# Another place for the split weights, one for each pair of gate and up groups

## The chip, the cores and the metric

The kernel runs on one core of a Trainium2 chip. The metric is the device time of one execution in microseconds (us). A profile of one execution shows TensorE (PE for its matmuls, PEld for its weight loads), VectorE (DVE), ScalarE (ACT), GpSimd (POOL) and the DMA queue of SyncE (SP).

## What is computed

Two layers of a hybrid block on one sequence of 256 tokens with 2,048 features, in float32. Each layer does an input projection, three mixers side by side (a spatial gate, a sliding-window attention and an mLSTM), an output projection, and a gated feed-forward block with 5,632 hidden features:

```
def hybrid_layer(x, ...):
    hn = rmsnorm(x, norm1_g)
    proj = hn @ w_in
    a_u, a_v, b_q, b_k, b_v, c_qk, c_v, c_o, c_i, c_f = jnp.split(proj, split_idx, axis=-1)
    ...
    mixed = jnp.concatenate([mix_a, mix_b, mix_c], axis=-1)
    h = x + mixed @ w_out
    hn2 = rmsnorm(h, norm2_g)
    return h + (jax.nn.silu(hn2 @ w_gate) * (hn2 @ w_up)) @ w_down
```

A last `rmsnorm` follows the second layer.

## The kernel before

**Products in two parts.** Every float32 weight and every activation is split into a high part (rounded to the type float32r, which TensorE multiplies in one pass) and a low part, the remainder. A product is the sum of high times high, high times low and low times high. The weights come from HBM in chunks of 4 x 128 rows by 512 columns. `wsplit` takes half a chunk (1,024 words of each partition): ScalarE writes the high part (`wh`, L206) and then VectorE subtracts it from the raw weight and writes the low part (`wl`, L207). Each of the two tiles `wh` and `wl` has four blocks of 1,024 words (`NSPLIT` = 4), used in turn; a block can be written again when the matmuls that read it have ended.

**Three forms.** Each product (a "group": 512 output columns over all the rows of the weight) is one call of `gemm` in one of three forms. In form A the activation is the stationary operand and the weights' part, 512 columns of it, is moved through the array (L262 to L264: three matmuls for each 128 rows and each half of the tokens). In forms B and C a 128 x 128 piece of the weights' part is stationary and the activation is moved. Form C uses two matmuls for a piece: L280 with the high part of the weights against 512 columns (both parts of the activation), and L281 with the low part against 256 columns. I call the two a pair. While one matmul runs, the stationary operand of the next one is loaded. Form B (L284 to L286) has three matmuls of 256 columns.

**Who uses which.** In each layer the groups run in this order: conv inputs `G_CQ` and `G_CK` (form B in layer 0, C in layer 1), the small group of 264 columns (A), `G_CV`, `G_Q0`, `G_Q1`, `G_AV` (A), `G_AU` (B), `G_CO` (A), 4 groups of the output projection (C), then twice: gate and up groups (12 the first time, 10 the second; C) and 4 groups of the down projection (C, but A the last time in layer 1). The 22 gate and up groups of a layer have 64 pairs each. Two consecutive ones are a "pair of groups", 11 of them, numbered 0 to 10 here.

**Places.** Within each block the parts don't begin at word 0 but at an offset that depends on the form alone, in words of 4 bytes, first for `wh`, then for `wl`:

```
LINE = 32
PLACE = dict(A=(20, 20), B=(12, 12), C=(24, 28))
```

The built program puts `wh` at byte 108,672 and `wl` at byte 125,184 of each partition, the activation `xn_sb` at 35,712, the four `big` tiles (which hold gated activations) at 141,696, 192,128, 200,320 and 208,512, and ten `slot` tiles every 4,224 bytes from 149,888. Counted modulo 256 bytes, `xn_sb` and all `big` tiles begin at 128, the slots by turns at 128 and 0; the blocks of `wh` and `wl` in form C at 224 and 112, in form A at 208 and 80. Where a product reads activations from slots, the profile's rows name them `slot`. In the first down projection of layer 1 the first two slots that are read begin at 128, the other two at 0, modulo 256; in the second down projection of layer 0 the two slots that are read begin at 0 and 128, two pairs each by turns; in the last down projection of layer 1 both begin at 0.

**Order.** Splits are issued with a high priority, and the scheduler puts each instruction into its engine's queue when what it depends on is scheduled. Dependences are found by the words that instructions read and write.

Of the kernel before, what the change touches and what calls it, by code (L numbers as in the profile page):

```python
# [8 lines left out]
F32R = mybir.dt.float32r  # L9
# [4 lines left out]
P = 128  # L14
# [13 lines left out]
CW = 512  # L28
WK = 4
SK = 2  # L30
# [9 lines left out]
LINE = 32  # L40
PLACE = dict(A=(20, 20), B=(12, 12), C=(24, 28))
NSPLIT = 4
# [6 lines left out]
OFF = dict(a_u=0, a_v=512, b_q=1024, b_k=2048, b_v=2176, c_q=2304, c_k=2816, c_v=3328, c_o=3840, c_i=4352, c_f=4356)  # L49
G_CQ, G_CK, G_CV, G_Q0, G_Q1, G_AV, G_AU, G_CO = range(8)  # L50
GROUP_COLS = [OFF["c_q"], OFF["c_k"], OFF["c_v"], OFF["b_q"], OFF["b_q"] + 512, OFF["a_v"], OFF["a_u"], OFF["c_o"]]


_p = 0
# [18 lines left out]
def hybrid(ctx: ExitStack, tc: tile.TileContext, xt, wfirst, win, wsm, wout, wgu, wdn, prm, cst, fgb, yt):  # L73
# [8 lines left out]
    wp = ctx.enter_context(tc.tile_pool(name="wp", bufs=1))  # L82
# [32 lines left out]
    def bank():  # L115
        return pm.tile([P, 512], F32, tag="m", name=nm("m"))
# [5 lines left out]
    def kchunks(w, order=None):  # L122

        order = range(KT // WK) if order is None else order
        return [(w[c], list(range(c * WK, (c + 1) * WK))) for c in order]
# [66 lines left out]
            load_next()  # L192
        return loaded[i]

    parts = [wp.tile([P, NSPLIT * SK * CW + LINE], F32R, tag=k, name=k) for k in ("wh", "wl")]
    split_no = [0]
    last_split = [None]

    def wsplit(raw, lo, n, form, pieces=1):
        i = split_no[0] % NSPLIT  # L200
        split_no[0] += 1
        wh, wl = [t[:, i * SK * CW + o:(i + 1) * SK * CW + o] for t, o in zip(parts, PLACE[form])]
        m = n // pieces
        with tc.high_priority(HIPRI):
            for i in range(0, n, m):
                A.copy(wh[:, i:i + m], raw(lo + i, m))  # L206
                last_split[0] = V.tensor_tensor(wl[:, i:i + m], raw(lo + i, m), wh[:, i:i + m].bitcast(F32),  # L207
                                                op=ALU.subtract)
        return wh, wl
# [9 lines left out]
    def gemm(*args, **kw):  # L219

        steps = gemm_steps(*args, **kw)
        while True:
            try:
                next(steps)
            except StopIteration as end:
                return end.value
# [9 lines left out]
                    out[i] = end.value  # L236
        return [out[i] for i in range(len(steps))]

    def gemm_steps(form, chunks, xs, cols=CW, ready=None, step0=SK, split=0):

        ps = [bank(), bank()] if split else gbank()
        if form == "C":
            up = [bank(), bank()]
            tiles = [ps[:, 0:512], ps[:, 512:1024], up[0], up[1]]  # L250
        nk = sum(len(k) for _, k in chunks)
        done = 0

        def mm_a(wh, wl, j, kt, first, last, cs=range(NC)):
            xh, xl = xs(kt)
            h = wh[:, j * cols:(j + 1) * cols]
            lo = wl[:, j * cols:(j + 1) * cols]
            for c in cs:
                o = ps[c][:, 0:cols] if split else ps[:, c * 512:c * 512 + cols]
                xhc = xh[:, c * P:(c + 1) * P]  # L260
                xlc = xl[:, c * P:(c + 1) * P]
                T.matmul(o, xhc, h, start=first, stop=False)  # L262
                T.matmul(o, xhc, lo, start=False, stop=False)  # L263
                T.matmul(o, xlc, h, start=False, stop=last)  # L264

        def mm_first(wh, wl, kt):

            xh, xl = xs(kt)
            for i, (w, x) in enumerate(((wh, xh), (wh, xl), (wl, xh))):
                for f in range(4):  # L270
                    T.matmul(ps[:, f * S:(f + 1) * S], w[:, f * P:(f + 1) * P], x, start=i == 0 and f % 2 == 0,
                             stop=False, skip_group_check=True)

        def mm_f(wh, wl, j, kt, f, first, last):
            xh, xl = xs(kt)
            h = wh[:, j * CW + f * P:j * CW + (f + 1) * P]
            lo = wl[:, j * CW + f * P:j * CW + (f + 1) * P]
            if form == "C":
                o = tiles[f]
                T.matmul(v3(o, 2), h, xs(kt, True), start=first, stop=False, skip_group_check=True)  # L280
                T.matmul(o[:, 0:S], lo, xh, start=False, stop=last, skip_group_check=True)  # L281
            else:
                o = ps[:, f * S:(f + 1) * S]
                T.matmul(o, h, xh, start=first and f % 2 == 0, stop=False, skip_group_check=True)  # L284
                T.matmul(o, h, xl, start=False, stop=False, skip_group_check=True)  # L285
                T.matmul(o, lo, xh, start=False, stop=last, skip_group_check=True)  # L286

        second = []
        for ci, (src, kts) in enumerate(chunks):
            apart = ci >= len(chunks) - split  # L290
            raw, step = wload(src, len(kts) * cols), step0 if ci == 0 else SK
            late = form != "A" and ci == len(chunks) - 1
            held = []
            for s0 in range(0, len(kts), step):
                ks = kts[s0:s0 + step]
                wh, wl = wsplit(raw, s0 * cols, len(ks) * cols, form, 2 if done == 0 and ready is ready_x else 1)
                if ready is not None:
                    ready(ks)
                for j, kt in enumerate(ks):
                    first, last = done == 0, done == nk - 1  # L300
                    done += 1
                    if form == "A":
                        mm_a(wh, wl, j, kt, first, last, range(1) if apart else range(NC))
                        if apart:
                            second.append((wh, wl, j, kt, first, last))
                    elif late:
                        held.append((wh, wl, j, kt, first, last))
                    elif first and ready is ready_x:
                        mm_first(wh, wl, kt)
                    else:  # L310
                        for f in range(4):
                            mm_f(wh, wl, j, kt, f, first, last)
                if not late:
                    pump()
                if step0 == 1 and ci == 0 and s0 + step < len(kts):
                    yield
            if late:
                for f in range(4):
                    for wh, wl, j, kt, first, last in held:
                        mm_f(wh, wl, j, kt, f, first, last)  # L320
                    if f % 2 == 1:
                        pump()
            if ci < len(chunks) - 1:
                yield
        for a in second:
            mm_a(*a, range(1, NC))
        return (ps, up[0], up[1]) if form == "C" else ps
# [29 lines left out]
    for g in range(2):  # L357
        for d in range(2):
            o = slice((1 - d) * HD, (2 - d) * HD)
# [632 lines left out]
    for l in range(DEPTH):  # L992
# [1 line left out]
        st = {}  # L994

        def inproj(i, form):
            return gemm(form, kchunks(win[l, i]), xn)

        if l == 0:
            start(rstd_of(st, True))  # L1000
            ps, ps1 = in_turn(gemm_steps("B", kchunks(win[l, G_CQ]), xn, ready=ready_x, step0=1),
                              gemm_steps("B", kchunks(win[l, G_CK]), xn, step0=1))
        else:
            start(rstd_of(st))
            ps = inproj(G_CQ, "C")
# [3 lines left out]
        ps = ps1 if l == 0 else inproj(G_CK, "C")  # L1009
        start(conv(st, "kc", scaled_in(ps, rbc), pr("conv"), 4))  # L1010
        ks, vn, gt = small_in(gemm("A", kchunks(wsm[l]), xn, cols=SMALL), rstd, pr)
# [10 lines left out]
        ps = inproj(G_AU, "B")  # L1022
        mixed[0] = big()
        start(gmlp_u(st, ps, rbc, mixed[0]))
        ps = inproj(G_CO, "A")
# [19 lines left out]
        for half, (c0, c1) in enumerate(HALVES):  # L1045
# [3 lines left out]
            for g in range(ng):  # L1049
                if half == 0 and g == 0:  # L1050
                    st = {}
                    start(rstd_of(st))
                ps = gemm("C", kchunks(wgu[l, 2 * c0 + g]), xn)
                need(st, "rbc")
                rbc = st["rbc"]
                ts = slot()
                t = ts[:, 0:1024]
                joined(t, ps)
                V.tensor_tensor(v3(t, 4), v3(t, 4), bc4(rbc), op=ALU.mult)
                A.activation(t[:, 0:512], t[:, 0:512], AF.Silu)  # L1060
                V.tensor_tensor(t[:, 0:512], t[:, 0:512], t[:, 512:1024], op=ALU.mult)
                if g >= 2 * NBIG:
                    a = slot(F32R)
                    small_act.append(a)
                    av = a[:, 0:1024].rearrange("p (k i t) -> p k i t", k=2, i=2)
                else:
                    if g % 2 == 0:
                        pair = big()
                    av = pair[:, 2 * (g % 2):2 * (g % 2) + 2]
                A.copy(av[:, :, 0, :], v3(t[:, 0:512], 2))  # L1070
                V.tensor_tensor(av[:, :, 1, :], v3(t[:, 0:512], 2), av[:, :, 0, :].bitcast(F32), op=ALU.subtract)
                release(ts)
                act.append(av)
# [112 lines left out]
```

## Time and profile before

| what | us |
|---|---|
| median of 3 runs (lowest, highest) | 2096.72 (2096.36, 2098.51) |
| the profiled execution | 2095.96 |
| its span, first to last instruction | 2094.1 |
| PE busy in it | 2081.6 |
| DVE busy | 1352.4 |
| ACT busy | 1022.9 |

The profiled execution is 1.9 us longer than its span (work around the program), and 0.8 us shorter than the median. The mean granted clock of TensorE was 0.999 of full speed. A row of the timeline gives the start of a matmul in us from the span's start; matmuls overlap in the array, so what one costs is read from start to start, not from its duration.

### The profile page before, as it was taken

How to read it: one execution, taken by the hardware profiler on the slowest of the kernel's cores; microseconds unless marked ns; L12 is line 12 of the kernel's file. 1: busy time of each engine (PE TensorE's matmuls, PEld its weight loads, DVE VectorE, ACT ScalarE, POOL GpSimd, SP SyncE). 2: the span in 40 equal slices, each digit the busy share in tenths (PEclk: the TensorE clock that was granted, in tenths of full speed). 3: DMA queues.
4: the chain of work that ended last, by engine and by line, in shares of the span. 5: the costliest groups of instructions: out<-in, count | busy, mean ns of one | idle time of the engine just before them, and what ended most of it. 6: DMA issues, size and time to landing. Idle time of an engine off the chain costs nothing.

```text
span 2094.1 us, 29478 instructions
## 1 busy us (share of the span) xinstructions
PE 2081.6 (99%) x12004; PEld 1824.8 (87%) x12004; DVE 1352.4 (65%) x1876; ACT 1022.9 (49%) x1350; POOL 9.1 (0%) x14
## 2 busy tenths in 40 slices
PE   9999999999999999999999999999999999999998
PEld 9888888888888888888888888888888888888886
DVE  7776666656654556566677865765665555656695
ACT  5665545444443345444455654454544434445443
POOL 0000000000000000000000000000000000000000
PEclk9999999999999999999999999999999999999999
DMA  6544555555555555555545435555555555555553
GB/s 253 210 144 148 181 188 194 185 197 184 199 187 195 182 200 183 199 183 200 185 160 199 144 138 192 190 188 195 187 195 193 189 191 191 196 186 196 206 194 128
DMA packets 56296, 390.47 MB, mean 186 GB/s; under 512 B 6496, under 2 KB 7008, under 8 KB 10080
## 3 DMA queue, kind: packets, MB, share of 16 engines
q1 hardware_dynamic: 55872, 388.06, 52.1%
q8 instruction: 94, 1.54, 0.3%
q10 hardware_dynamic: 288, 0.52, 0.1%
q14 instruction: 42, 0.34, 0.0%
HBM read 386.47 MB, written 2.10 MB: 186 GB/s over the span
## 4 chain that ended last, share of the span: by engine, by line
PE 98%; ACT 1%; DVE 0%; issue 0%; DMA 0%; SPq 0%; POOLq 0%; POOL 0%; DVEq 0%; ACTq 0%
PE g L280 25%; PE m L280 25%; PE g L281 13%; PE m L281 13%; PE g L262 5%; PE g L263 5%; PE g L264 5%; PE g L284 1%; PE g L286 1%; PE g L285 1%; PE m L608 1%; PE m L662 1%; PE m L651 1%; PE m L262 0%; PE m L263 0%; PE m L264 0%
## 5 line engine op out<-in xcount | busy, mean ns | idle before, releaser
L207 DVE TENSOR_TENSOR wl<-raw,wh 128x1024 fp32r<-128x1024 f32 (+2 forms) x741 | 886.5, 1205 | 579.3 <-ACT wh L206 576.1
L206 ACT CAST wh<-raw 128x1024 fp32r<-128x1024 f32 (+2 forms) x741 | 758.7, 1034 | 816.6 <-PE m L280 577.7
L280 PE MATMUL g<-xn_sb,wh 128*128 128x512 f32 x1472 | 534.8, 390 | 0.0
L280 PE MATMUL m<-xn_sb,wh 128*128 128x512 f32 x1472 | 533.7, 390 | 0.0
L281 PE MATMUL g<-xn_sb,wl 128*128 128x256 f32 x1472 | 409.6, 278 | 0.0
L281 PE MATMUL m<-xn_sb,wl 128*128 128x256 f32 x1472 | 409.6, 278 | 0.0
L280 PEld LDWEIGHTS m<-xn_sb,wh 128*128 128x128 f32 x1472 | 276.3, 188 | 58.0
L280 PEld LDWEIGHTS g<-xn_sb,wh 128*128 128x128 f32 x1472 | 276.3, 188 | 57.9
L281 PEld LDWEIGHTS g<-xn_sb,wl 128*128 128x128 f32 x1472 | 276.3, 188 | 0.2
L281 PEld LDWEIGHTS m<-xn_sb,wl 128*128 128x128 f32 x1472 | 276.3, 188 | 0.0
L280 PE MATMUL g<-big,wh 128*128 128x512 f32 x640 | 234.2, 390 | 0.0
L280 PE MATMUL m<-big,wh 128*128 128x512 f32 x640 | 233.9, 390 | 0.0
L281 PE MATMUL g<-big,wl 128*128 128x256 f32 x640 | 178.3, 279 | 0.0
L281 PE MATMUL m<-big,wl 128*128 128x256 f32 x640 | 178.3, 279 | 0.0
L262 PE MATMUL g<-wh,xn_sb 128*128 128x512 f32 (+1 forms) x384 | 146.5, 381 | 0.0
L263 PE MATMUL g<-wl,xn_sb 128*128 128x512 f32 (+1 forms) x384 | 144.2, 376 | 0.0
L264 PE MATMUL g<-wh,xn_sb 128*128 128x512 f32 (+1 forms) x384 | 143.4, 373 | 0.0
L280 PEld LDWEIGHTS m<-big,wh 128*128 128x128 f32 x640 | 120.2, 188 | 25.5
L280 PEld LDWEIGHTS g<-big,wh 128*128 128x128 f32 x640 | 120.2, 188 | 25.4
L281 PEld LDWEIGHTS g<-big,wl 128*128 128x128 f32 x640 | 120.2, 188 | 0.1
L281 PEld LDWEIGHTS m<-big,wl 128*128 128x128 f32 x640 | 120.2, 188 | 0.0
L264 PEld LDWEIGHTS g<-wh,xn_sb 128*128 128x128 f32 x384 | 72.3, 188 | 13.9
(238 smaller groups left out, 2098.7 us busy)
## 6 DMA issues: line engine op xcount, KB each, us to landing
raw<-in_wgu SPq DMA_DIRECT2D x176, 1024.0 KB, 4.7
raw<-in_wdn SPq DMA_DIRECT2D x88, 1024.0 KB, 4.7
raw<-in_win SPq DMA_DIRECT2D x62, 1024.0 KB, 4.8
raw<-in_wout SPq DMA_DIRECT2D x32, 1024.0 KB, 4.7
raw<-in_wsm SPq DMA_DIRECT2D x8, 528.0 KB, 3.2
out_yt<-end SPq DMA_DIRECT2D x4, 384.0 KB, 3.0
raw<-in_wfirst SPq DMA_DIRECT2D x2, 512.0 KB, 6.9
hT<-in_xt SPq DMA_DIRECT2D x1, 1024.0 KB, 14.2
```

The source lines that it names most:

```text
L206: A.copy(wh[:, i:i + m], raw(lo + i, m))
L207: last_split[0] = V.tensor_tensor(wl[:, i:i + m], raw(lo + i, m), wh[:, i:i + m].bitcast(F32), op=ALU.subtract)
L262: T.matmul(o, xhc, h, start=first, stop=False)
L263: T.matmul(o, xhc, lo, start=False, stop=False)
L264: T.matmul(o, xlc, h, start=False, stop=last)
L280: T.matmul(v3(o, 2), h, xs(kt, True), start=first, stop=False, skip_group_check=True)
L281: T.matmul(o[:, 0:S], lo, xh, start=False, stop=last, skip_group_check=True)
L284: T.matmul(o, h, xh, start=first and f % 2 == 0, stop=False, skip_group_check=True)
L285: T.matmul(o, h, xl, start=False, stop=False, skip_group_check=True)
L286: T.matmul(o, lo, xh, start=False, stop=last, skip_group_check=True)
L608: T.matmul(o, q2[d][:, sl], k[:, 0:n], start=i == 0, stop=i == 1, skip_group_check=True)
L651: T.transpose(b[:, p * P:(p + 1) * P], pslice(c, 2 * p + par)[:, blk * P:(blk + 1) * P], ident)
```

## The change

It gives a place of its own to each pair of gate and up groups (`GU_PLACE`, the same in both layers) and to ten groups of form A (`A_PLACE`, five in each layer). All other groups keep `PLACE`. `wl` gets 64 more words at its end, so that every tile that stands behind it (slots, `big` tiles, small tiles) moves up by 256 bytes.

```diff
+GU_PLACE = ((24, 60), (24, 44), (24, 92), (23, 28), (25, 28), (24, 27), (24, 29), (25, 29), (23, 27), (22, 26), (20, 24))
+A_PLACE = ({G_CV: (32, 32), G_Q0: (19, 19), G_Q1: (20, 32), G_AV: (32, 20), G_CO: (31, 31)},
+           {G_CV: (30, 30), G_Q0: (18, 20), G_Q1: (20, 84), G_AV: (20, 52), G_CO: (0, 0)})
...
-    parts = [wp.tile([P, NSPLIT * SK * CW + LINE], F32R, tag=k, name=k) for k in ("wh", "wl")]
+    parts = [wp.tile([P, NSPLIT * SK * CW + n * LINE], F32R, tag=k, name=k) for k, n in (("wh", 1), ("wl", 3))]
...
-    def wsplit(raw, lo, n, form, pieces=1):
+    def wsplit(raw, lo, n, place, pieces=1):
...
-        wh, wl = [t[:, i * SK * CW + o:(i + 1) * SK * CW + o] for t, o in zip(parts, PLACE[form])]
+        wh, wl = [t[:, i * SK * CW + o:(i + 1) * SK * CW + o] for t, o in zip(parts, place)]
...
-    def gemm_steps(form, chunks, xs, cols=CW, ready=None, step0=SK, split=0):
+    def gemm_steps(form, chunks, xs, cols=CW, ready=None, step0=SK, split=0, place=None):
...
-                wh, wl = wsplit(raw, s0 * cols, len(ks) * cols, form, 2 if done == 0 and ready is ready_x else 1)
+                wh, wl = wsplit(raw, s0 * cols, len(ks) * cols, place or PLACE[form], 2 if done == 0 and ready is ready_x else 1)
...
-            return gemm(form, kchunks(win[l, i]), xn)
+            return gemm(form, kchunks(win[l, i]), xn, place=A_PLACE[l].get(i))
...
-                ps = gemm("C", kchunks(wgu[l, 2 * c0 + g]), xn)
+                ps = gemm("C", kchunks(wgu[l, 2 * c0 + g]), xn, place=GU_PLACE[c0 + g // 2])
```

The number, the shapes and the order of TensorE's instructions stay as they are. Where a group's place lies further on than that of the group ahead, a new block runs a few words into the next block, which older matmuls still read; so its split waits for those too, and the scheduler puts it later. In the gate and up groups the order on ScalarE and VectorE stays as it is. Around form A it moves.

On ScalarE, before, in layer 0 between the small group and `G_CV` (the casts of 528 columns are the small group's, the first of 1,024 is `G_CV`'s; the `ACTIVATE` on `slot_653` and `slot_662` are silu on conv outputs):

```order
L206 CAST wh<-raw 128x528 x2
L206 CAST wh<-raw 128x1024
L504 ACT_TABLE_LOAD
L504 ACTIVATE slot_653<-slot_653 128x1024
L206 CAST wh<-raw 128x1024 x4
L504 ACTIVATE slot_662<-slot_662 128x1024
```

The same place with the change, where lines have moved by 5:

```order
L211 CAST wh<-raw 128x528 x2
L509 ACT_TABLE_LOAD
L509 ACTIVATE slot_653<-slot_653 128x1024
L211 CAST wh<-raw 128x1024 x2
L509 ACTIVATE slot_662<-slot_662 128x1024
L211 CAST wh<-raw 128x1024 x2
```

The first cast of `G_CV` has moved behind the table load and one silu, its third behind the second silu.

On VectorE, before, at the same place (the `SCALAR_TENSOR_TENSOR` rows are taps of the conv):

```order
L500 SCALAR_TENSOR_TENSOR slot_653<-slot_633,prm_90,slot_653 128x253
L500 SCALAR_TENSOR_TENSOR slot_662<-slot_635,prm_90,slot_662 128x255 x2
L207 TENSOR_TENSOR wl<-raw,wh 128x1024
L500 SCALAR_TENSOR_TENSOR slot_662<-slot_635,prm_90,slot_662 128x254 x2
L207 TENSOR_TENSOR wl<-raw,wh 128x1024 x3
L500 SCALAR_TENSOR_TENSOR slot_662<-slot_635,prm_90,slot_662 128x253 x2
```

With the change:

```order
L505 SCALAR_TENSOR_TENSOR slot_653<-slot_633,prm_90,slot_653 128x253
L505 SCALAR_TENSOR_TENSOR slot_662<-slot_635,prm_90,slot_662 128x255 x2
L505 SCALAR_TENSOR_TENSOR slot_662<-slot_635,prm_90,slot_662 128x254 x2
L505 SCALAR_TENSOR_TENSOR slot_662<-slot_635,prm_90,slot_662 128x253 x2
L212 TENSOR_TENSOR wl<-raw,wh 128x1024 x2
```

`G_CV`'s first subtraction has moved behind four more taps of the conv.

## Rows read from the trace of the kernel before

**Rows 1.** The page: span, busy time (share) xinstructions, chain that ended last.
```profile
span 2094.1 us, 29478 instructions
PE 2081.6 (99%) x12004; PEld 1824.8 (87%) x12004; DVE 1352.4 (65%) x1876; ACT 1022.9 (49%) x1350; POOL 9.1 (0%) x14
...
PE 98%; ACT 1%; DVE 0%; issue 0%; DMA 0%; SPq 0%; POOLq 0%; POOL 0%; DVEq 0%; ACTq 0%
```

**Rows 2.** PE's waits: us in total, times, longest us.
```profile
PE g L286 <- DVE wl L207: 1.1, 4, 0.4
```

**Rows 3.** Timeline of PE, gate and up group 3 of layer 0: start, us, engine.
```profile
387.00 0.39 PE L280 MATMUL g<-xn_sb,wh 128*128 128x512 f32 x1
387.35 0.39 PE L280 MATMUL g<-xn_sb,wh 128*128 128x512 f32 x1
...
408.98 0.39 PE L280 MATMUL g<-xn_sb,wh 128*128 128x512 f32 x1
```

**Rows 4.** That group's window: length, PE PEld DVE ACT POOL busy (instructions), clock, DMA.
```profile
387.00:408.98 21.98, 21.98 (x131) 19.46 (x129) 13.50 (x14) 10.68 (x14) 0.00 (x0) 1.00 0.55 192
```

**Rows 5.** Timeline of PE, first down projection of layer 1, the slots' pairs.
```profile
1644.84 0.39 PE L280 MATMUL g<-slot,wh 128*128 128x512 f32 x1
...
1650.33 0.39 PE L280 MATMUL g<-slot,wh 128*128 128x512 f32 x1
...
1655.91 0.39 PE L280 MATMUL g<-big,wh 128*128 128x512 f32 x1
```

**Rows 6.** Timeline of PE, second group of layer 0's first down projection.
```profile
617.92 0.39 PE L280 MATMUL g<-big,wh 128*128 128x512 f32 x1
...
640.39 0.41 PE L280 MATMUL g<-slot,wh 128*128 128x512 f32 x1
```

**Rows 7.** Timeline of PE, layer 0's second down projection, slots by turns.
```profile
960.03 0.39 PE L280 MATMUL g<-slot,wh 128*128 128x512 f32 x1
...
960.73 0.39 PE L280 MATMUL g<-slot,wh 128*128 128x512 f32 x1
...
961.41 0.39 PE L280 MATMUL g<-slot,wh 128*128 128x512 f32 x1
```

**Rows 8.** Timeline of PE, layer 1's last down projection, form A.
```profile
1974.79 0.39 PE L262 MATMUL g<-wh,big 128*128 128x512 f32 x1
...
1996.87 0.40 PE L262 MATMUL g<-wh,slot 128*128 128x512 f32 x1
...
1999.67 0.40 PE L262 MATMUL g<-wh,slot 128*128 128x512 f32 x1
```

**Rows 9.** Timeline of PE, the small group of form A in layer 0.
```profile
54.67 0.28 PE L262 MATMUL g<-wh,xn_sb 128*128 128x264 f32 x1
...
55.41 0.29 PE L262 MATMUL g<-wh,xn_sb 128*128 128x264 f32 x1
...
56.13 0.28 PE L262 MATMUL g<-wh,xn_sb 128*128 128x264 f32 x1
```

**Rows 10.** Timelines of ACT, DVE and PE where layer 0's `G_CV` begins.
```profile
62.15 1.05 ACT L206 CAST wh<-raw 128x1024 fp32r<-128x1024 f32 x1 [0.77 <-PE g L264]
63.22 1.28 ACT L504 ACT_TABLE_LOAD   x1
64.51 1.07 ACT L504 ACTIVATE slot<-slot 128x1024 f32<-128x1024 f32 x1
...
62.16 1.66 DVE L500 SCALAR_TENSOR_TENSOR slot<-slot,prm,slot 128x253 f32<-128x253 f32 x4
63.74 1.22 DVE L207 TENSOR_TENSOR wl<-raw,wh 128x1024 fp32r<-128x1024 f32 x1
64.88 0.87 DVE L500 SCALAR_TENSOR_TENSOR slot<-slot,prm,slot 128x254 f32<-128x254 f32 x2
...
66.30 0.39 PE L262 MATMUL g<-wh,xn_sb 128*128 128x512 f32 x1
66.53 0.39 PE L263 MATMUL g<-wl,xn_sb 128*128 128x512 f32 x1
```

## The prediction

> **What bounds the kernel now.** I read the page first. PE is busy for 99% of the span and holds 98% of the chain that ended last [rows 1], so only what lengthens or shortens PE's own stream of matmuls, or makes it wait, can move the time. The view of waits shows little to win there: its largest entry for the weights' parts is four waits of 1.1 us together [rows 2].
>
> The next view is PE's timeline, read from start to start. Gate and up group 3 of layer 0 runs from 387.00 to 408.98, 21.98 us for 64 pairs, 343.4 ns a pair [rows 3]. In it TensorE's granted clock is at the upper of its levels throughout (1.00, so 2.4 GHz) [rows 4]. If each of a pair's 768 columns took one cycle of it, a pair would take 320 ns (an estimate): some 23 ns (7%) go to something else. DVE is busy for 13.50 and ACT for 10.68 of the 21.98 us [rows 4], so neither holds PE up; the 23 ns are PE's own.
>
> So the question is whether those 23 ns hang on where the operands stand. The rows say yes. In the first down projection of layer 1 the parts of the weights stand as in the gate and up groups, and the moved activation comes from slots. Sixteen pairs with slots that begin at 128, modulo 256 bytes, take 1650.33 - 1644.84 = 5.49 us, 343.1 ns each; the next sixteen, with slots at 0, take 5.58 us, 348.8 ns each [rows 5]. Same columns, same lines, 5.7 ns more. In form A the stationary operand is the activation: 96 matmuls with `big` tiles (at 128) take 22.08 us, 230.0 ns each, and 12 with slots at 0 take 2.80 us, 233.3 ns each [rows 8]. There only the stationary address changed. And the small group steps its moved part by 32 bytes from one 264 columns to the next: 6 matmuls take 0.74 us, the next 6 take 0.72 [rows 9], some 3 ns a matmul.
>
> Address is not all of it. In layer 0, 64 pairs with `big` tiles take 640.39 - 617.92 = 22.47 us, 351.1 ns each [rows 6], with the parts at the usual places. The stream can settle into a slower rhythm at the same residues and stay there for a whole group.
>
> **The change, part by part.** Gate and up: 22 groups x 64 pairs x 2 layers are 2,816 pairs, and each of the eleven places holds 256 of them. 1 ns on one place is 0.26 us; 1 ns on all is 2.8 us.
>
> Place 0, (24, 60): the low part, the one loaded during the 512-column matmul, moves by 128 bytes. Against the moved operand that is the shift which [rows 5] show from the other side: 5.7 ns x 256 = 1.5 us. Bounds: nothing, if only the moved operand's own address counts, and 7.7 ns (351.1 - 343.4, [rows 6]), 2.0 us.
>
> Place 1, (24, 44): 64 bytes, half of that shift. No row has it; between 0 and 5.7 ns I take the middle, 2.8 ns, 0.7 us.
>
> Place 2, (24, 92): 256 bytes. What [rows 5] and [rows 8] tell apart are residues modulo 256, which this place keeps; I take nothing, bounds as for place 0.
>
> Places 3 to 10 shift one or both parts by 4 to 16 bytes. No row shows so small a step. Below, the bound is the fastest stretch in the trace: two pairs with the slot at 0 take 0.70 us, the two with the slot at 128 take 0.68 [rows 7], so 340 to 343 ns with the rounding, a gain of at most 3.4 ns. Above it is 7.7 ns again. The nearest row is the step of 32 bytes [rows 9], 3 ns a matmul; a smaller step should do less. The place of before sits near the fast end of what the trace shows (340 to 351), so a step from it has more room upwards: I take 1.5 ns. 8 x 256 x 1.5 ns = 3.1 us.
>
> Form A: ten groups x 96 matmuls. Here the parts are the moved operand. Rows of this form lie between 230.0 and 233.3 ns [rows 8] and the small group shows 3 ns in either direction [rows 9], so 960 x 3.3 ns = 3.2 us up or down; with steps in both directions I take 0.
>
> The tiles behind `wl` move up by 256 bytes, which keeps every residue modulo 256: 0.
>
> The order: no matmul moves, but splits wait longer where a place moves on. In the gate and up groups the first splits of a new place wait for one more pair (0.34 us), and the first two blocks are free once five and six of the eight splits of the group ahead have run, 8.2 and 5.5 us (3/8 and 2/8 of 21.98) before that group ends: hidden. The one place with little cover is `G_CV`. There ACT is free at 62.15 - 0.77 = 61.38; the table load takes 1.28; the silu needs two of the four taps that DVE begins at 62.16 (1.66 us for four), so it starts near 63.0 and ends at 64.07; the first cast follows until 65.12. DVE does the four taps until 63.82 and four more (two times 0.87) until 65.56, then the subtraction (1.22) until 66.78. PE wants the high part at 66.30 and the low part at 66.53 [rows 10]. So PE waits about 0.25 us, with G_CV's next matmuls behind it. I take the same for layer 1. Bounds: nothing, and a whole subtraction in each layer, 2.4 us. Before `G_AV` a cast falls behind six exponentials, with several us in hand: 0. Sum: 0.5 us.
>
> All together 1.5 + 0.7 + 0 + 3.1 + 0 + 0 + 0.5 = 5.8 us. On the profiled execution (2095.96, span and what lies around it) that is 2101.8; the median of the runs is 0.8 us above that execution, so 2102.5.
>
> **A rule against this.** Form A moves the same operand at two speeds for two stationary addresses [rows 8]. The Trainium skill ("TensorE: Matmul & The Clock Gate", Part 2, the step on loading the stationary operand) says that PE reads the stationary and the moved operand through two independent ports, and that loading the next weights takes no read bandwidth from the running matmul. By that rule the eleven gate and up places would cost nothing and the sum would be the order's and form A's alone; the trace's 233.3 against 230.0 ns speaks against it.
>
> **The rivals.**
>
> Stationary places don't matter (the change does nothing there). Then [rows 5] tell only of the moved operand, and [rows 8] of something else in the slots. For it: 351.1 ns in [rows 6] at unchanged residues shows that address is not the only cause. Against it: only the stationary operand differs within [rows 8]. Time: 2096.7 + 0.5 = 2097.2, with form A 2094 to 2100.
>
> The slow rhythm. If six of the eleven places lock the stream at 351.1 ns, that is 6 x 256 x 7.7 ns = 11.8 us, the other five at 1.5 ns add 1.9, the order 0.5: 2111. For it: [rows 6], a whole stretch at the usual places. Against it: the gate and up groups keep to 343.4 [rows 3].
>
> Faster. The stream settles at the fast end, 341.7 ns (the middle of 340 to 343.4), on average over all eleven places: -1.7 ns x 2,816 = -4.8 us, so 2092 to 2093 with the order's 0.5. It decides from an average below 341.9 ns (4.2 us over 2,816 pairs). For it: [rows 7]. Against it: that takes a gain at nearly every place, while the wide shifts point the other way.
>
> **How the numbers follow.** 0.2% of 2096.7 us is 4.2 us, about what a measurement of this kernel can tell from no change: 2092.5 and 2100.9 are the limits. The forecast gets 0.50, with its own range 2099 to 2106, of which 0.08 lies under the limit; no effect of stationary places 0.25; the slow rhythm 0.17; faster 0.08, of which 0.01 stays within the limit. Slower: 0.42 + 0.17 = 0.59. Same: 0.08 + 0.25 + 0.01 = 0.34. Faster: 0.07. The range runs from 2095 (no effect, with form A gaining) to 2112 (the slow rhythm at six places); below it lies the faster case, above it more than six slow places.
>
> **What would show it.** In the changed profile each gate and up group's length from first pair to first pair gives its place's price: place 0 near 22.3 us instead of 21.98, place 2 still 21.98, places 3 to 10 between 21.8 and 22.4, the same in both layers. Form A's groups should stay within 3 ns a matmul of 230. DVE's `wl` at `G_CV` should end near 66.8, with a wait of some tenths. I am wrong if all groups stay at 21.98; if a place that starts on a word outside the usual grid costs 10 ns or more a pair; or if a moved part of form A at an odd word slows its whole stream, for which no row gives a bound as near as these. A slower cast or subtraction at such places would not show in the time until a subtraction takes (21.98 - 13.50 + 8 x 1.22) / 8 = 2.28 us.

## The result, and the profile after

The changed kernel takes 2115.63 us (median of 4 runs, 2115.52 to 2116.58), the kernel before 2096.54 us beside it (4 runs, 2096.05 to 2098.51): 1.0092 times as long, interval 1.0079 to 1.0105. It is 19 us slower, where 5.8 were forecast. The profiled execution took 2115.52 us.

The page of the changed kernel answers to [rows 1]: span, busy time (share) xinstructions, and the chain that ended last.

```profile
span 2113.7 us, 29470 instructions
...
PE 2102.0 (99%) x12004; PEld 1833.2 (87%) x12004; DVE 1351.9 (64%) x1876; ACT 1022.0 (48%) x1350; POOL 9.1 (0%) x14
...
PE 97%; DVE 1%; DMA 1%; issue 0%; SPq 0%; ACT 0%; POOLq 0%; DVEq 0%; POOL 0%; ACTq 0%
```

The span is 19.6 us longer and PE's busy time 20.4, with the same 12,004 matmuls; DVE and ACT are as busy as before. So PE does the same work at another pace. Its largest waits, 1.1, 1.0 and 0.9 us, are about those of before, 1.1 us three times.

The windows of the changed kernel, one row for one group of each place in layer 0, in the order of the places 0 to 10 (the columns are those of [rows 4]):

```profile
344.00:366.44 22.44, 22.44 (x130) 19.59 (x129) 13.59 (x14) 11.85 (x15) 0.00 (x0) 1.00 0.52 180
366.44:388.77 22.33, 22.33 (x131) 19.62 (x129) 13.50 (x14) 10.66 (x14) 0.00 (x0) 1.00 0.52 189
411.10:433.08 21.98, 21.98 (x130) 19.45 (x129) 13.50 (x14) 10.66 (x14) 0.00 (x0) 1.00 0.53 187
455.06:477.56 22.50, 22.50 (x130) 19.63 (x129) 13.51 (x14) 10.68 (x14) 0.00 (x0) 1.00 0.54 191
500.07:522.57 22.50, 22.50 (x130) 19.51 (x129) 13.51 (x14) 10.68 (x14) 0.00 (x0) 1.00 0.55 196
545.08:567.50 22.42, 22.42 (x131) 19.63 (x129) 13.50 (x14) 10.68 (x14) 0.00 (x0) 1.00 0.53 184
723.48:746.09 22.61, 22.61 (x131) 19.61 (x130) 11.51 (x12) 9.26 (x11) 0.00 (x0) 1.00 0.54 187
768.70:790.89 22.19, 22.19 (x130) 19.56 (x129) 13.52 (x14) 10.66 (x14) 0.00 (x0) 1.00 0.54 195
813.08:835.41 22.33, 22.33 (x130) 19.57 (x129) 13.51 (x14) 10.67 (x14) 0.00 (x0) 1.00 0.52 191
857.75:880.34 22.59, 22.59 (x131) 19.78 (x129) 13.50 (x14) 10.68 (x14) 0.00 (x0) 1.00 0.54 191
902.95:925.14 22.19, 22.19 (x130) 19.51 (x129) 13.51 (x14) 10.66 (x14) 0.00 (x0) 1.00 0.53 190
```

Before, every gate and up group was 21.97 us long (group 3 in [rows 3, 4], the others from the trace) but the first of each layer, which holds four other matmuls and took 22.86; now only place 2 still has that length. The granted clock is 1.00 in each row, PE is busy throughout, and each length comes back in layer 1 within 0.02 us. Summed over the 44 gate and up groups, from trace times, the excess is 17.6 of the span's 19.6 us: 1.9 at place 0, 1.4 at place 1, nothing at place 2, 14.3 at places 3 to 10. The other 2.0 lie in the other groups: 0.7 in the down projections, which kept their place, 0.6 in form A, 0.4 in the conv inputs, 0.3 in the output projections. The 0.4 is not shown to be the change's: the small group behind the conv inputs begins at 54.7 us before and at 55.1 in the changed kernel, but at 53.6 and at 55.4 in the first two runs below, and the conv inputs have the same places in all four.

Around `G_CV` of layer 0, the timelines of ACT, DVE and PE of the changed kernel answer to [rows 10]:

```profile
63.45 1.06 ACT L509 ACTIVATE slot<-slot 128x1024 f32<-128x1024 f32 x1 [0.39 <-DVE slot L505]
64.41 1.98 ACT L211 CAST wh<-raw 128x1024 fp32r<-128x1024 f32 x2
...
65.69 2.37 DVE L212 TENSOR_TENSOR wl<-raw,wh 128x1024 fp32r<-128x1024 f32 x2
...
66.68 0.39 PE L267 MATMUL g<-wh,xn_sb 128*128 128x512 f32 x1
66.97 0.50 PE L268 MATMUL g<-wl,xn_sb 128*128 128x512 f32 x1
67.31 0.39 PE L269 MATMUL g<-wh,xn_sb 128*128 128x512 f32 x1
```

From start to start the first two matmuls take 0.29 and 0.34 us instead of some 0.23, so PE waits 0.17 us here. In layer 1 the same matmuls are 0.23 to 0.24 apart: no wait.

### The profile page after: what moved, and what is told of

It reads as the page before. It is cut to its first block, busy times and chain, and to the rows that moved or that the text cites. A ratio compares the mean times of both kernels' runs of the same rounds, so it can differ in the third digit from the quotient of the medians.

```text
span 2113.7 us, 29470 instructions
## 1 busy us (share of the span) xinstructions
PE 2102.0 (99%) x12004; PEld 1833.2 (87%) x12004; DVE 1351.9 (64%) x1876; ACT 1022.0 (48%) x1350; POOL 9.1 (0%) x14
## 4 chain that ended last, share of the span: by engine, by line
PE 97%; DVE 1%; DMA 1%; issue 0%; SPq 0%; ACT 0%; POOLq 0%; DVEq 0%; POOL 0%; ACTq 0%
PE g L285 25%; PE m L285 25%; PE m L286 13%; PE g L286 13%; PE g L267 5%; PE g L268 5%; PE g L269 5%; PE g L289 1%; PE g L291 1%; PE g L290 1%; PE m L613 1%; DMA raw<-in_win 1%; PE m L667 1%; PE m L656 1%; PE m L267 0%
## 5 line engine op out<-in xcount | busy, mean ns | idle before, releaser
L285 PE MATMUL g<-xn_sb,wh 128*128 128x512 f32 x1472 | 541.9, 394 | 0.0
L285 PE MATMUL m<-xn_sb,wh 128*128 128x512 f32 x1472 | 540.7, 394 | 0.0
L285 PEld LDWEIGHTS m<-xn_sb,wh 128*128 128x128 f32 x1472 | 276.6, 188 | 63.8
L285 PEld LDWEIGHTS g<-xn_sb,wh 128*128 128x128 f32 x1472 | 276.6, 188 | 63.6
L285 PE MATMUL g<-big,wh 128*128 128x512 f32 x640 | 234.7, 391 | 0.0
L285 PE MATMUL m<-big,wh 128*128 128x512 f32 x640 | 234.5, 391 | 0.0
L285 PEld LDWEIGHTS m<-big,wh 128*128 128x128 f32 x640 | 120.2, 188 | 25.7
L285 PEld LDWEIGHTS g<-big,wh 128*128 128x128 f32 x640 | 120.2, 188 | 25.6
```

## The experiments

The first theory is the prediction's: the gate and up places cost the time, the shift behind `wl` nothing. The rivals that came up on the way were that a place has a price of its own, counted from the moved operand or by its own address, and last that the stream has a few rhythms and that the way a group is entered helps to choose one. The expectations number them as they came up; below they are told in words. Where no number of executions is given, there is one. A place is called usual when it is that of before, (24, 28) for the gate and up groups. Line numbers differ by a few between these kernels.

**The shift alone, and form A alone** (`shift_only`, `a_only`, 10 executions each).

```diff
 # shift_only
-GU_PLACE = ((24, 60), (24, 44), ...
-A_PLACE = ({G_CV: (32, 32), ...
+GU_PLACE = ((24, 28),) * 11
+A_PLACE = ({}, {})
 # a_only: only the change of GU_PLACE, A_PLACE as in the change
```

> Only the 64 words behind the low part stay (all tiles behind it 256 bytes further), every group at its usual place. Theory 1 (the price of a place is all in the gate and up groups): within 1.5 us of before, every gate and up group at 21.97 us. Rival (the tiles behind moved, and that brought the slow rhythm): most of the 19 us is here too, and gate and up groups longer than 22.1 us.

> The ten places of form A and the shift by 256 bytes, the gate and up groups at (24, 28). Theory 1: 0 to 2 us above before, gate and up groups at 21.97 us; form A's groups and the waits at G_CV as in the changed kernel. Rival (reordered splits in form A start the slow rhythm, which the gate and up groups inherit): over 10 us above before.

`shift_only`: 2096.3 us against 2096.43, ratio 1.000 (0.999 to 1.0009). `a_only`: 2097.29, ratio 1.0004 (0.9995 to 1.0014). In both all gate and up groups but the first of each layer are 21.97 us long, and those take 22.84 to 22.86. The windows of one group of `shift_only`, and of the same one of `a_only`:

```profile
385.87:407.84 21.97, 21.97 (x130) 19.44 (x129) 13.50 (x14) 10.68 (x14) 0.00 (x0) 1.00 0.55 192
```

```profile
387.70:409.68 21.98, 21.98 (x131) 19.45 (x130) 13.50 (x14) 10.69 (x14) 0.00 (x0) 1.00 0.54 192
```

The shift is worth nothing and form A with its order at most 0.14% (2.9 us); in the profile form A's groups are 0.6 us longer, as in the changed kernel. The gate and up places are left.

**The same places in reverse order** (`gu_reversed`, 4 executions; here and in all runs below form A has its usual places).

```diff
-                ps = gemm("C", kchunks(wgu[l, 2 * c0 + g]), xn, place=GU_PLACE[c0 + g // 2])
+                ps = gemm("C", kchunks(wgu[l, 2 * c0 + g]), xn, place=GU_PLACE[10 - (c0 + g // 2)])
```

> The eleven gate and up places in the reverse order, form A at its usual places. Theory 1 (a place has its price wherever it stands): each place keeps the length of its groups in the changed kernel within 0.03 us, so (24, 60) 22.45 at the end and (20, 24) 22.19 at the start; in all 17.6 us above before plus the shift's share. Rival (the price belongs to the stretch of the program or to the group ahead): the lengths stay with the number of the group, or move by more than 0.1 us.

2113.48 us, ratio 1.0081 (1.0066 to 1.0096). Seven of the eleven places keep their lengths in both layers. Four don't. Windows of a group at (22, 26), in layer 0 and in layer 1, and of a group at (24, 92), in the same two layers:

```profile
365.43:388.02 22.59, 22.59 (x130) 19.78 (x129) 13.50 (x14) 10.68 (x14) 0.00 (x0) 1.00 0.54 196
1435.11:1457.72 22.61, 22.61 (x130) 19.80 (x129) 13.51 (x14) 10.67 (x14) 0.00 (x0) 1.00 0.52 180
812.45:834.93 22.48, 22.48 (x130) 19.70 (x129) 13.50 (x14) 10.68 (x14) 0.00 (x0) 1.00 0.55 194
1858.61:1880.59 21.98, 21.98 (x130) 19.46 (x129) 13.50 (x14) 10.66 (x14) 0.00 (x0) 1.00 0.56 193
```

(22, 26) costs what it did. (24, 92), which cost nothing in the changed kernel, costs 0.5 us in layer 0 and nothing in layer 1; (24, 29) fell from 22.61 to 22.19 in both. So a place mostly brings its own length, but not always.

**The moved activation one word further** (`xn_one_word`; in layer 0 all parts one word further with it, in layer 1 the parts as in the change).

```diff
-    xn_sb = cp.tile([P, KT, 2, S], F32R, tag="xn", name="xn_sb")
+    xn_flat = cp.tile([P, KT * 2 * S + LINE], F32R, tag="xn", name="xn_sb")
+    xn_sb = xn_flat[:, 1:1 + KT * 2 * S].rearrange("p (a b c) -> p a b c", a=KT, b=2)
...
-                ps = gemm("C", kchunks(wgu[l, 2 * c0 + g]), xn, place=GU_PLACE[c0 + g // 2])
+                ps = gemm("C", kchunks(wgu[l, 2 * c0 + g]), xn, place=[o + 1 - l for o in GU_PLACE[c0 + g // 2]])
```

> The moved activation of the gate and up groups begins one word (4 bytes) further. In layer 0 both parts of every place of the table are one word further too, in layer 1 the table is as it was; form A at its usual places. Theory 2 (what counts is where the parts stand relative to the moved operand): layer 0 repeats the changed kernel's lengths within 0.05 us (22.45, 22.33, 21.98, 22.51, 22.51, 22.42, 22.61, 22.19, 22.33, 22.59, 22.19) and layer 1 does not. Theory 3 (what counts is the parts' own address, such as a start off a 16-byte line): layer 1 repeats them and layer 0 does not. If neither repeats, both count.

2144.24 us. Windows of group 2 in layer 0 and in layer 1 (place 1):

```profile
368.90:391.93 23.03, 23.03 (x131) 19.92 (x129) 13.51 (x14) 10.68 (x14) 0.00 (x0) 1.00 0.51 182
1431.85:1454.88 23.03, 23.03 (x131) 20.02 (x130) 13.51 (x14) 10.68 (x14) 0.00 (x0) 1.00 0.54 185
```

Neither layer repeats the lengths of the change (22.33 there): about half of the groups are near 23.04 us, 360 ns a pair, and none is under 22.6. A moved operand that begins one word further than usual costs by itself: 48 us in all over the kernel before, where the change alone costs 19. The second conv input of layer 1 shows it best, because its parts stay at the usual place; it takes 23.04 us instead of 21.97:

```profile
1095.73:1118.77 23.04, 23.04 (x131) 19.85 (x129) 16.19 (x25) 11.55 (x18) 0.00 (x0) 1.00 0.31 100
```

The distance from the activation doesn't explain it: (23, 27) has the same distance in the changed kernel and took 22.33. Neither kind of price list was to be seen through this cost.

**128 places on the grid of 16 bytes** (`scan_a`, `scan_b`, `scan_c`: `wh` at 0 to 28, `wl` at 0 to 60 words in steps of 4, in random order, a place for each group).

```diff
-GU_PLACE = ((24, 60), (24, 44), ...
+GU_PLACE = (
+    (8, 12), (20, 48), (4, 0), (16, 44), (16, 56), (16, 4), (0, 12), (20, 24), (8, 8), (16, 60), (28, 8),
...
-                ps = gemm("C", kchunks(wgu[l, 2 * c0 + g]), xn, place=GU_PLACE[c0 + g // 2])
+                ps = gemm("C", kchunks(wgu[l, 2 * c0 + g]), xn, place=GU_PLACE[NGU * l + 2 * c0 + g])
```

> Each of the 44 gate and up groups has a place of its own, the high part at a multiple of 4 words from 0 to 28, the low part at a multiple of 4 from 0 to 60, in an arbitrary order; the last has the usual place. First third of the 128 such places. Theory 4 (the usual place is at the fast end of a wide spread, so almost any step costs): the groups lie between 21.9 and 22.7 us, their mean near 22.35, at most one in ten within 0.02 of 21.97. Rival (starts on multiples of 16 bytes are all as fast as the usual one, and only the starts between cost): all within 0.05 of 21.97, but for the two that the changed kernel already had.

> The second third of the 128 places. As for the first: theory 4 mean near 22.35 and at most one in ten at 21.97; the rival all near 21.97.

> The last third of the 128 places, and the usual place at the end. As for the first: theory 4 mean near 22.35 and at most one in ten at 21.97; the rival all near 21.97.

2115.92, 2115.3 and 2115.05 us. Windows of `scan_c`, at (16, 28), (16, 36), (24, 28), (16, 32), (20, 12), and at (24, 28) once more at its end:

```profile
388.70:410.88 22.18, 22.18 (x131) 19.58 (x129) 13.51 (x14) 10.66 (x14) 0.00 (x0) 1.00 0.55 196
522.56:544.32 21.76, 21.76 (x130) 19.31 (x129) 13.51 (x14) 10.66 (x14) 0.00 (x0) 1.00 0.52 183
544.32:566.29 21.97, 21.97 (x130) 19.45 (x129) 13.51 (x14) 10.68 (x14) 0.00 (x0) 1.00 0.54 195
811.65:834.05 22.40, 22.40 (x131) 19.67 (x130) 13.51 (x14) 10.68 (x14) 0.00 (x0) 1.00 0.53 188
1836.45:1859.06 22.61, 22.61 (x131) 19.54 (x129) 13.50 (x14) 10.67 (x14) 0.00 (x0) 1.00 0.56 193
1971.46:1993.93 22.47, 22.47 (x130) 19.70 (x129) 13.50 (x14) 10.67 (x14) 0.00 (x0) 1.00 0.51 187
```

The lengths are not spread evenly. 85 of 121 groups at other places than the usual (the first group of each layer left out) lie within 0.02 us of one of 21.76, 22.19, 22.40 and 22.61; 30 of the other 36 lie at 22.27 to 22.36 or at 22.43 to 22.53. The usual place has 21.97 or 22.47. The steps between 21.76, 21.97, 22.19, 22.40 and 22.61 are 0.21 us for 64 pairs, 3.33 ns a pair, which is 8 cycles of the 2.4 GHz that the granted clock of 1.00 means. The mean is 22.38: over 44 groups (22.38 - 21.97) x 44 = 18 us, which is what the change lost. Two places are faster than the usual one, (16, 4) and (16, 36). Places with both parts at multiples of 32 bytes are no better: 22.42 in the mean of 30.

The third and the last row are one place with two lengths: 21.97 and 22.47, the second being the 351.1 ns a pair of [rows 6].

**The activation four words further** (`xn_four_words`, 44 places).

```diff
...
+    xn_sb = xn_flat[:, 4:4 + KT * 2 * S].rearrange("p (a b c) -> p a b c", a=KT, b=2)
...
```

> The moved activation begins 4 words (16 bytes) further; 44 places at multiples of 4 words, (24, 28) and (28, 32) among them. Theory 2 (relative to the moved operand): a group's length is that of the place 4 words less in both parts in the scan without the shift, so (28, 32) takes 21.97 and (24, 28) about 22.19. Theory 3 (own addresses of the parts): lengths by the scan at the same place, (24, 28) 21.97. Theory 3b (the moved operand's own start counts most, as with one word): all groups over 22.5 whatever the place.

2114.3 us, a mean length of 22.37. Four words further, the moved operand costs nothing on average (22.38 in the scans). Compared place by place, the lengths go neither with the same distance from the activation (correlation 0.16 with the scans) nor with the same address (0.3). (28, 32), which has the distance that (24, 28) usually has, took 22.61 us and not 21.97; (24, 28) itself took 22.19 both times. So a list with one price for each distance, or for each address, falls.

**One place for a whole layer** (`one_place_16`, 4 executions; `one_place_odd`, one).

```diff
 # one_place_16
...
+GU_PLACE = ((16, 4),) * 22 + ((16, 36),) * 22
 # one_place_odd
...
+GU_PLACE = ((24, 29),) * 22 + ((25, 29),) * 22
```

> All 22 gate and up groups of layer 0 at (16, 4), all of layer 1 at (16, 36), the two places whose groups took 21.77 us in the scans. Theory 5 (PE's stream settles into one of a few rhythms, 340.0, 343.3, 346.7, 350.0 ... ns a pair; a place says which of them it can hold, the way into the group picks one): all groups of a layer in one rhythm, 21.77 us if it is the one of the scans, and then 44 x 0.21 = 9 us below before, about 2087.5. Theory 4 alone (a place has one price): the same 21.77. If the rhythm of the scans was an accident of the entry: 22.19 or 22.40 throughout, 9 to 19 us above before.

> All groups of layer 0 at (24, 29), all of layer 1 at (25, 29). (24, 29) took 22.61 in the changed kernel and 22.19 in the reversed one, (25, 29) 22.19 in both. Theory 5: layer 0 in one of these two from its second group to its last, layer 1 at 22.19; no group at 21.97. Rival (it is the change of place that costs, a place held throughout returns to 21.97): all near 21.97 after the first.

`one_place_16`: **2087.0 us** (4 runs, 2086.74 to 2087.51), ratio 0.9955 (0.9938 to 0.9972), faster than both kernels. `one_place_odd`: 2115.74 us; all groups but the first of a layer are 22.61 in layer 0 and 22.19 in layer 1, as these two places were in the changed kernel. The page and PE's timeline of `one_place_16`, from the start of a group:

```profile
span 2085.3 us, 29473 instructions
...
PE 2073.6 (99%) x12004; PEld 1818.6 (87%) x12004; DVE 1351.9 (65%) x1876; ACT 1022.5 (49%) x1350; POOL 9.1 (0%) x14
```

```profile
386.81 0.39 PE L284 MATMUL g<-xn_sb,wh 128*128 128x512 f32 x1
387.04 0.28 PE L285 MATMUL g<-xn_sb,wl 128*128 128x256 f32 x1
387.15 0.39 PE L284 MATMUL g<-xn_sb,wh 128*128 128x512 f32 x1
387.38 0.28 PE L285 MATMUL g<-xn_sb,wl 128*128 128x256 f32 x1
```

And the windows of `one_place_odd`, one group of each layer:

```profile
366.50:389.12 22.62, 22.62 (x131) 19.61 (x129) 13.51 (x14) 10.67 (x14) 0.00 (x0) 1.00 0.51 185
1417.94:1440.13 22.19, 22.19 (x130) 19.57 (x129) 13.51 (x14) 10.69 (x14) 0.00 (x0) 1.00 0.55 188
```

In the trace's nanoseconds, 64 matmuls of L284 from 365 to 387 us in `one_place_16` take 227 each and 64 of L285 take 113 each, without one exception. At the usual place a turn repeats only after three pairs: of 63 matmuls of 512 columns in one group of `shift_only` 21 take 227, 21 take 228, 11 take 226 and 10 take 229. In the rhythm of 22.47 us (the last group of `scan_c`) every third takes 241, throughout. Splits run on DVE for 13.50 us of each group, and in these groups the pace is the same while they run and while they don't: a split that comes in PE's way is not what sets it.

In these two runs a whole layer at one place keeps one length. The step of one word from the usual place that lost 0.2 or 0.6 us in the changed kernel loses it again in every group.

**The usual place, entered in other ways** (`usual_kicked`: ahead of each gate and up group one more matmul of 4 to 232 columns into a bank that the group then overwrites).

```diff
...
+        if form == "C" and place is not None:
+            kicks[0] += 1
+            T.matmul(up[0][:, 0:4 + 12 * (kicks[0] % 20)], kbh[0][:, 0:P], kbh[0][:, 0:4 + 12 * (kicks[0] % 20)], start=True,
+                     stop=True, skip_group_check=True)
...
```

> The usual place (24, 28) in every gate and up group, and one small matmul more ahead of each group's first pair (4 to 232 columns, into a bank that the group then overwrites), so that each group is entered at another moment. Theory 5: the first pair is shifted, and some of the 44 groups go to 22.47 us (351.1 ns a pair, the rhythm that the scans showed at this place three times), the others stay at 21.97; nothing else. Rival (address alone): all at 21.97, but for the added matmul's 0.02 to 0.2 us.

2107.36 us. PE's timeline where groups 9 and 10 of layer 0 are entered (L260 is the extra matmul), and the windows of groups 8, 9 and 10 there and of group 7 in layer 1, each up to the first pair of the next:

```profile
520.50 0.22 PE L260 MATMUL m<-kbh 128*128 128x124 f32 x1
520.56 0.45 PE L289 MATMUL g<-xn_sb,wh 128*128 128x512 f32 x1
...
543.09 0.23 PE L260 MATMUL m<-kbh 128*128 128x136 f32 x1
543.15 0.45 PE L289 MATMUL g<-xn_sb,wh 128*128 128x512 f32 x1
543.43 0.28 PE L290 MATMUL g<-xn_sb,wl 128*128 128x256 f32 x1
```

```profile
498.46:520.56 22.10, 22.10 (x131) 19.57 (x131) 13.50 (x14) 10.69 (x14) 0.00 (x0) 1.00 0.54 195
520.56:543.15 22.59, 22.59 (x131) 19.82 (x131) 13.50 (x14) 10.69 (x14) 0.00 (x0) 1.00 0.53 187
543.15:565.25 22.10, 22.10 (x131) 19.57 (x131) 13.50 (x14) 10.68 (x14) 0.00 (x0) 1.00 0.53 186
...
1520.29:1542.88 22.59, 22.59 (x132) 19.80 (x131) 13.51 (x14) 10.69 (x14) 0.00 (x0) 1.00 0.52 190
```

Nothing but the way in differs. Nine of the 44 groups take 22.48 to 22.55 us (the extra matmul not counted), all others 21.97 to 22.08, but for the first of each layer. Group 9 of layer 0 and group 7 of layer 1 are the two with 124 columns ahead of them, and both are slow; so are both with 220 and both with 4 columns, two of the three with 28 and one of the two with 184. The way in picks between the place's two rhythms, and mostly picks the same again; by what rule is not shown.

**Every second group at one place** (`visits`: (16, 4) in layer 0 and (24, 28) in layer 1, other places between).

```diff
...
+GU_PLACE = (
+    (12, 36), (16, 4), (28, 4), (16, 4), (16, 32), (16, 4), (28, 0), (16, 4), (28, 36), (16, 4), (24, 20),
...
+    (4, 32), (24, 28), (4, 28), (24, 28), (24, 36), (24, 28), (28, 28), (24, 28), (12, 48), (24, 28), (20, 8),
```

> Every second group of layer 0 at (16, 4), every second of layer 1 at the usual (24, 28); between them 22 other places. Theory 5: the visits to one place fall into two or three lengths, (24, 28) into 21.97 and 22.47, (16, 4) into 21.77 and another one. Theory 4 alone: the 11 visits to one place agree within 0.03 us.

2107.79 us. Windows of groups 3 and 9 of layer 0, both at (16, 4), and 3 and 15 of layer 1, both at (24, 28):

```profile
387.95:409.71 21.76, 21.76 (x130) 19.25 (x129) 13.50 (x14) 10.64 (x14) 0.00 (x0) 1.00 0.55 190
520.34:542.74 22.40, 22.40 (x131) 19.64 (x129) 13.50 (x14) 10.66 (x14) 0.00 (x0) 1.00 0.52 180
1431.89:1453.87 21.98, 21.98 (x131) 19.45 (x130) 13.50 (x14) 10.68 (x14) 0.00 (x0) 1.00 0.55 197
1830.89:1853.37 22.48, 22.48 (x131) 19.72 (x130) 13.51 (x14) 10.69 (x14) 0.00 (x0) 1.00 0.53 186
```

Of 11 visits (16, 4) has 21.76 or 21.77 in six and 22.40 or 22.41 in five, while all groups behind the first had 21.76 or 21.77 where a whole layer kept to it; (24, 28) has 21.97 to 21.99 in ten and 22.47 in one. Each has two lengths and none between. The group ahead doesn't decide it by its own pace: after groups of 22.61 or 22.62 us (16, 4) came out fast once and slow twice.

## Why the prediction was wrong

**What bounds the kernel, and the sign.** Right. PE's own pace is what moved, at the upper clock: 17.6 of the span's 19.6 us lie in the gate and up groups, where nothing waits. The address of the stationary operand alone moves it: 340.0 ns a pair at (16, 4) and 353.3 at (24, 29), with the moved operand unchanged. The Trainium skill's rule of two independent ports ("TensorE: Matmul & The Clock Gate", Part 2) speaks of read bandwidth and not of addresses; that these places would be free, as the prediction drew from it, these rows do not bear out.

**The step that failed: places 3 to 10.** I took 1.5 ns a pair, 3.1 us, from the 32-byte step of [rows 9] with "a smaller step should do less". They measured (22.50 + 22.50 + 22.42 + 22.61 + 22.19 + 22.33 + 22.59 + 22.19 - 8 x 21.97) x 4 = 14.3 us, 3.4 to 10 ns a pair, 7.0 in the mean. The price does not shrink with the step: 4 bytes cost up to 10 ns a pair (place 6), 16 bytes in both parts 3.4 (place 10). Runs show in its place that most groups go in one of a few rhythms 8 cycles apart, that the usual place has the second fastest of those seen, and that an arbitrary place lands on average 0.41 us a group above it. Six of the eleven places lie within 0.03 us of such a rhythm; places 0, 1, 3, 4 and 8, at 22.33 to 22.51, lie between two, as the slow rhythm of [rows 6] does. The bound of 7.7 ns, taken from the slowest row, was no bound: four of these places lie above it, at 8.3 to 10 ns.

**Place 0 and place 1.** 1.5 us forecast, 1.9 measured; 0.7 forecast, 1.4 measured. The size at place 0 was near, but by luck: the ground for it, a shift of half of 256 bytes against the activation, is not borne out, since the lengths of `xn_four_words` don't follow the distance from the activation. **Place 2** cost nothing, as forecast, but in the reversed order it cost 0.5 us a group in layer 0, so the residue modulo 256 is not the rule either.

**Form A, the shift, the order.** Shift: 0, as measured. Form A: 0 forecast; 0.6 us in the profile, inside its bounds, and steps do go both ways: from trace times `G_CO` took 22.10 us before, in the change 21.97 with its moved parts at the odd words (31, 31) in layer 0 and 22.40 at (0, 0) in layer 1. So an odd word for the moved operand did not slow form A, as the prediction feared that it might and as it did in form C. Order: layer 0's wait was 0.17 us for 0.25, layer 1's, which I took to be the same, is not there.

**Other groups.** I gave nothing to groups that keep their place. The first down projection's first group in layer 1 takes 33.68 us instead of 33.05, and that is most of the 0.7 us in the down projections. The four in layer 0, which had 33.16 and 33.62 by turns, have them in the opposite order. The same happens in `gu_reversed` and not in `shift_only` or `a_only`, so it comes from the groups ahead: that these groups are entered otherwise is the likely reason. The turns also show that one place had two lengths in the kernel before already.

**The rivals.** The slow rhythm was the nearest, 2111 at 0.17, and had the mechanism in hand ("the stream can settle into a slower rhythm at the same residues"). It needed six places at 351.1 ns; ten of eleven went to 346.7 to 353.3 ns, and not all to one rhythm. I weighed it down because the gate and up groups had kept to 343.4, but they had kept their place too: [rows 3] couldn't speak of other places.

**What stays open.** Which relation of the addresses sets the rhythms that a place can have. The scans show no order in it that I found, and in form C the moved operand's own address counts too. How an entry picks between the rhythms of a place is open as well.

## What to carry to other kernels

When a stream of matmuls runs at a fixed pace that repeats exactly from group to group, look at it pair by pair: a place of its operands may be one of few lucky ones, and moving it is a draw, not a small step. Judge a place by the length that it gives to a whole run of groups, not by one visit, and keep a run of groups at one place; here one good place for each layer gained 9.4 us where eleven different ones lost 19, and one poor place for each layer lost 19 as well. And take the average over places that were drawn blindly, rather than the nearest row, as the price of leaving a tuned place.

## What was not expected of the hardware

With the granted clock at 1.00 a pair of 512 and 256 columns took 340.0, 343.3, 346.7, 350.0 or 353.3 ns on average over most groups; most others lay within about 1 ns of 348.9 or of 351.1, which at the usual place comes in turns of three pairs. In form C a moved operand that starts one word further than usual took 353 to 360 ns a pair at all stationary places tried, one that starts four words further 340 to 357. And one extra matmul ahead of a group, 0.06 us from its start to the next in the rows of `usual_kicked`, can change the pace of the 128 that follow.
